# Attention and the SSD half of the output projection in hand-written source order, on one Trainium2 core

## The chip, the core and the metric

The kernel runs on one core of a Trainium2 chip. A core has a matrix engine (TensorE, PE in the profile, with its weight loads as PEld), a vector engine (VectorE, DVE), an activation engine (ScalarE, ACT), a third elementwise engine (GpSimd, POOL), and a queue processor that only starts transfers (SyncE, SP). Each engine has a stream of instructions of its own. Operands lie in the core's SRAM; TensorE writes its sums to PSUM banks, and weights and some intermediate tensors travel to and from DRAM by DMA. The metric is the device time of one execution in microseconds (us); smaller is better.

## What is computed

One block of a hybrid model for 512 tokens of 2048 features, all in fp32. Cut to what matters:

```python
def reference(x, attn_norm_w, w_in, ..., w_out, ffn_norm_w, w_gate, w_up, w_down, final_norm_w):
    h = x
    u = rmsnorm(h, attn_norm_w)                                   # 512 x 2048
    z, xbc, dt, q, kc, vc, ks, vs, kw, vw, gate = split(u @ w_in) # in-projection, 2048 x 5184
    y_ssd = ssd_mixer(z, xbc, dt, ...)          # conv, chunked state space, rmsnorm(y * silu(z)): 512 x 1024
    y_att = nsa_mixer(q, kc, vc, ks, vs, kw, vw, gate, ...)       # 16 heads of 64, 4 key groups: 512 x 1024
    mixed = concatenate([y_ssd, y_att])
    h = h + mixed @ w_out                                         # out-projection, 2048 x 2048
    v = rmsnorm(h, ffn_norm_w)
    h = h + (silu(v @ w_gate) * (v @ w_up)) @ w_down              # FFN
    return rmsnorm(h, final_norm_w)
```

`nsa_mixer` adds three gated attentions: over 31 compressed keys (two small matrix products, w1 and w2, make them from kc and vc), over selected blocks and over a window. With 512 tokens the latter two are plain causal attentions with their own keys (branch 0: ks, vs; branch 1: kw, vw).

## The kernel before

**Split products.** Every fp32 operand is split into a high part and a remainder (`a_hi` on ACT, `lo` on DVE or POOL, the helpers at L120 and L123), and a product is three matmuls: high by high, high by low, low by high. A *unit* is 128 columns of a projection for all 512 tokens: 16 k-steps of three matmuls (L227 to L229) into one of two `ps_g` banks; a k-step is a *weight step*. There are 57 units: 41 of the in-projection (the last 19 are, beside three for z, the v, k and q columns of the four key groups) and then 16 of the SSD half of the out-projection with 8 k-steps each. A unit's weights come by SP in chunks of four k-steps (`wraw`), and are split into `whi` (ACT) and `wlo` (DVE), three chunks ahead (LEAD). When a unit is done, its `evac` scales the bank by `rrow` on DVE and goes on: rope and a split for q and k (`ev_q`, `ev_ks`), transposes for v (`ev_vs`), silu and a gate for z (`ev_z`), the residual sum and the squares for the next norm for the out-projection (`ev_os`).

**Ticks.** All work beside the units is written as Python generators under `Sched`: after each weight step `sch.tick()` advances every generator, and a generator says by `yield n` after how many weight steps it wants to go on. `compress` (the w1 and w2 products, L620 to L669) and `attention` are two of them. Attention goes through 32 items for each of four key groups: head h, branch br, row block i of 128 queries against 128(i+1) keys. An item is `score` (two matmuls into one of two `ps_s` banks, L830 and L831, then on DVE the masked maximum at L834, then on ACT the exponential with its sum at L836), `norm` (reciprocal L843 and scaling, on DVE alone or on ACT for branch 0), `trans` (i+1 transposes into one of two `ps_t` banks, L859, then `pth` on ACT and `ptl` on DVE), and after four items `pvmm` (eight matmuls with the values, L875, into the single `ps_v` bank, with the compressed branch at L869 and L870 ahead of branch 0). After two branches the head's output goes to `at`, and each pair of heads is one of eight operands of the second half of the out-projection.

**What sets the order.** In the kernel before, that source order is only the input: the stages up to the second half of the out-projection lie in one block, which the tile framework's list scheduler rearranges by its own simulation of the engines. The second half of the out-projection (L1160 to L1162; its weights are `Z`, loaded by SP, and `R`, split off on ACT) and the FFN come behind, in an order written by hand under `tc.manual_schedule()`. `pre_out` runs ahead of the first out-projection unit; it loads the eight gated SSD outputs `gy_d` and splits them.

The main loop of before, at the end of the body, is

```python
    for n, u in enumerate(units):
        if n == 4:
            ...
        run_unit(u)
    run_rest()
```

Of the kernel before, what the change touches and what calls it, by code (L numbers as in the profile page):

```python
# [26 lines left out]
KSUB = 4  # L27
PACE = [1]
LAG = 3
EB = 5  # L30
LEAD = 3
# [79 lines left out]
def body(ctx, tc, xT, w_in, w_out, w_gate, w_up, w_down, w1k, w1v, cols, rows, kst, out):  # L111
# [60 lines left out]


    subs = []

    class Unit:
        def __init__(self, src, nk, rhs, evac, need=(), pre=None, cols=(0, 512)):
            self.cols, self.rhs, self.evac, self.need, self.pre, self.nk = cols, rhs, evac, need, pre, nk
            self.sub = []
# [5 lines left out]
    st = {"dma": 0, "split": 0}  # L185
# [10 lines left out]
    def issue_split(upto):  # L196
        while st["split"] <= min(upto, len(subs) - 1):
# [3 lines left out]
            h = wp.tile([128, KSUB, 128], F32R, tag="whi", name="whi", bufs=4)  # L201
            l = wp.tile([128, KSUB, 128], F32R, tag="wlo", name="wlo", bufs=4)
            a_hi(h[:, :n, :], raw[i][:, :n, :])
            lo(dve, l[:, :n, :], raw[i][:, :n, :], h[:, :n, :])
            hi_t[i], lo_t[i] = h, l
            del raw[i]
            st["split"] += 1
            issue_dma(i + 3)

    def run_unit(u):  # L210
# [9 lines left out]
        for i, k0, n in u.sub:  # L220
            issue_split(i)
            for j in range(n):
                if j == 0:
                    issue_split(i + LEAD)
                k = k0 + j
# [4 lines left out]
                sch.tick()  # L230
            del hi_t[i], lo_t[i]

        def evac():
            yield from u.evac(p)
            sch.flags.add(("evac", n_u))
# [307 lines left out]
    def ev_z(t):  # L543
        def ev(p):
# [11 lines left out]
            else:  # L556
                yield from sch.wait("att")
                sp = pools["att"][1]
# [3 lines left out]
                mul(dve, zs, p, rrow)  # L562
                act.activation(zs, zs, AF.Silu)
                mul(pool, zs, zs, y)
            nc.gpsimd.dma_start(gy_d[t], zs)
            if t == 0:
                act.activation(acc2, zs, AF.Square)
            else:
                sq = sp.tile([128, 512], F32, tag="sq" if g == 0 else "yz", name="sq", bufs=1)
                act.activation(sq, zs, AF.Square)  # L570
                add(pool, acc2, acc2, sq)
            sch.flags.add(("gy", t))
# [105 lines left out]
    def ev_vs(g):  # L678
        def ev(p):
            yield from sch.wait("r1", "att")  # L680
            ap = pools["att"][1]
# [3 lines left out]
            yield from after(("a", g - 2))  # L685
            q = ps_m()
            for i in range(4):
                pe.transpose(q[:, i * 128:(i + 1) * 128], t[:, i * 128:(i + 1) * 128], ident)
            v = ap.tile([128, 4, 2, 128], F32R, tag="v", name="v", bufs=2)
            for br in range(2):  # L690
                s = q.rearrange("p (i b d) -> p i b d", i=4, b=2)[:, :, br, :]
                a_hi(v[:, :, br, 0:64], s)
                lo(dve, v[:, :, br, 64:128], s, v[:, :, br, 0:64])
# [17 lines left out]
    def rope2(ap, sw, ro):  # L711
        t = ap.tile([128, 512], F32, tag="fo", name="ro2", bufs=1)
# [3 lines left out]
    def ev_ks(g):  # L716
        def ev(p):
            yield from sch.wait("r1", "att")
            ap = pools["att"][1]
            t = ap.tile([128, 512], F32, tag="qs", name="kt", bufs=2)  # L720
            mul(dve, t, p, rrow)
            sw, ro = rope(ap, t)
            yield 4
            rope2(ap, sw, ro)
            yield from after(("a", g - 2))
            kh = ap.tile([128, 2, 512], F32R, tag="kh", name="kh", bufs=2)
            kl = ap.tile([128, 2, 512], F32R, tag="kl", name="kl", bufs=2)
            for br in range(2):
                s = ro[br * 64:br * 64 + 64, :]
                own = slice(br * 64, br * 64 + 64)  # L730
                for r in range(2):
                    d = slice(r * 64, r * 64 + 64)
                    a_hi(kh[d, br, :], s)
                for r in range(2):
                    d = slice(r * 64, r * 64 + 64)
                    lo(dve if r == br else pool, kl[d, br, :], s, kh[own, br, :])
            R["k", g] = (kh, kl)
# [3 lines left out]
    def q_stack(ap, tag, bufs, s, eng):  # L741
        t = ap.tile([128, 2, 512], F32R, tag=tag, name=tag, bufs=bufs)
        a_hi(t[0:64, 0, :], s[0:64, :])
        a_hi(t[64:128, 1, :], s[64:128, :])
        lo(eng, t[64:128, 0, :], s[0:64, :], t[0:64, 0, :])
# [3 lines left out]
    def ev_q(g, j):  # L749
        def ev(p):  # L750
            yield from sch.wait("r1", "att")
            ap = pools["att"][1]
            t = ap.tile([128, 512], F32, tag="qs", name="qt", bufs=2)
            mul(dve, t, p, rrow)
            sw, ro = rope(ap, t)
            uq = q_stack(ap, "uq", 1, t, pool)
            yield 2
            yield from after(("sc", g - 2))
            if j == 0:
                R["sc", g] = ap.tile([128, 4, 4, 32], F32, tag="sc", name="sc", bufs=2)  # L760
            m = ps_m()
            pv = m[:, 0:256].rearrange("p (i h k) -> p i h k", i=4, h=2)
            for i in range(4):
                for h in range(2):
                    st_ = uq[:, h, i * 128:(i + 1) * 128]
                    pe.matmul(pv[:, i, h, :], st_, kch[:, g, :], start=True, stop=False)
                    pe.matmul(pv[:, i, h, :], st_, kcl[:, g, :], start=False, stop=True)
            dve.tensor_tensor(R["sc", g][:, :, 2 * j:2 * j + 2, :], pv,
                              cmask[:, :, None, :].to_broadcast([128, 4, 2, 32]), ALU.add)
            yield 2  # L770
            rope2(ap, sw, ro)
            if (g, j) == (3, 1):
# [4 lines left out]
                sch.flags.add("x")  # L777
            yield from after(("h", g - 1 if j else g - 2, 1 if j else 3))
            R["rq", g, j] = q_stack(ap, "rq", 3, ro, dve)
# [3 lines left out]
    def attention():  # L783
# [6 lines left out]
        for g in range(4):  # L790
# [10 lines left out]
                              ALU.subtract)  # L801
            act.activation(sc, sc, AF.Exp, scale=0.125)
            for h in range(4):
                a_hi(vpad[32 * h:32 * h + 32, h, 0:64], vcmp[:, g, :])
                lo(dve, vpad[32 * h:32 * h + 32, h, 64:128], vcmp[:, g, :], vpad[32 * h:32 * h + 32, h, 0:64])
# [10 lines left out]
            sch.flags.add(("sc", g))  # L816
            ch = ap.tile([128, 512], F32R, tag="cph", name="cph", bufs=1)
            cl = ap.tile([128, 512], F32R, tag="cpl", name="cpl", bufs=1)
            a_hi(ch, p)
            lo(dve, cl, p, ch)  # L820
# [4 lines left out]

# [962 lines left out]
```

## Time and profile before

| | |
|---|---|
| median of 3 runs | 2290.25 us (2285.53 to 2290.41) |
| the profiled execution | 2288.18 us |
| its span in the trace | 2286.4 us |
| mean granted TensorE clock | 0.977 of full speed |
| PE busy | 2186.6 us, 96% of the span |
| DVE busy | 1804.6 us, 79% |
| ACT busy | 1091.9 us, 48% |
| POOL busy | 431.1 us, 19% |

The span is counted from its own start, and all places below are us from there. The last unit matmul starts at 777.42, the second half of the out-projection at 800.12, and the FFN takes the rest. A matmul's recorded duration is longer than the spacing of matmuls, since they are pipelined; where work is counted, the spacing is used. A wait is put down to the releaser that came last. The granted clock is a mean over a stretch: it is 1.00 at 2.4 GHz and 0.5 at 1.2 GHz, and values between are a mixture.

### The profile page before, as it was taken

The numbers are of one execution on the slowest core, as the hardware profiler recorded it, in microseconds if no ns is written. First come the engines' busy times: TensorE is split into PE (matmuls) and PEld (weight loads), VectorE is DVE, ScalarE is ACT, GpSimd is POOL, SyncE is SP. The second block draws the span as 40 slices with busy tenths as digits, with TensorE's granted clock in tenths as the row PEclk, the third lists the DMA queues.
The fourth block names the chain that finished last, engine by engine and source line by source line (L and its number), as shares of the span: only waits on it lengthen the run. The fifth ranks groups of instructions, "written<-read, shape, count | busy, mean of one in ns | idle before, by whom it ended". The sixth has DMA issues, their size and how long they took to land. (4 is left out here: it accounts for less than half of the span.)

```text
span 2286.4 us, 39808 instructions
## 1 busy us (share of the span) xinstructions
PE 2186.6 (96%) x15376; PEld 2039.4 (89%) x15376; DVE 1804.6 (79%) x2921; ACT 1091.9 (48%) x1770; POOL 431.1 (19%) x436
## 2 busy tenths in 40 slices
PE   7999999999989899999999999999999698989997
PEld 5888888888868678999999999999999698989996
DVE  7699766688888667888887888888887687878786
ACT  4564446566766544444444444444444233333353
POOL 2011334223233133100000000000001121212132
PEclk8999999999999899999999999999999899999998
DMA  5222343222424265878787887878788758677776
GB/s 176 92 70 77 129 135 104 69 85 74 135 63 137 73 226 158 244 218 243 213 255 220 249 227 221 238 218 244 220 255 255 285 173 264 207 241 234 247 169 168
DMA packets 151693, 417.87 MB, mean 183 GB/s; under 512 B 16352, under 2 KB 22000, under 8 KB 151504
## 3 DMA queue, kind: packets, MB, share of 16 engines
q1 hardware_dynamic: 99408, 251.25, 31.6%
q0 software_dynamic: 25536, 77.05, 17.5%
q10 hardware_dynamic: 26560, 87.04, 10.6%
q8 instruction: 120, 1.97, 0.3%
q14 instruction: 69, 0.57, 0.1%
HBM read 353.93 MB, written 57.41 MB: 180 GB/s over the span
## 5 line engine op out<-in xcount | busy, mean ns | idle before, releaser
L120 ACT ACTIVATE R<-Z 128x1024 fp32r<-128x1024 f32 (+4 forms) x488 | 441.9, 922 | 575.0 <-DVE Z L129 324.6
L123 DVE TENSOR_TENSOR R<-Z,R 128x1024 fp32r<-128x1024 f32 (+4 forms) x381 | 395.2, 1043 | 26.1 <-ACT R L120 20.4
L227 PE MATMUL ps_g<-u,whi 128*128 128x512 f32 x720 | 286.1, 397 | 0.2 <-DVE h L126 0.2
L229 PE MATMUL ps_g<-u,wlo 128*128 128x512 f32 x720 | 284.5, 395 | 0.0
L228 PE MATMUL ps_g<-u,whi 128*128 128x512 f32 x720 | 283.9, 394 | 0.0
L1160 PE MATMUL ps_g<-u,R 128*128 128x256 f32 (+1 forms) x834 | 250.7, 301 | 7.6 <-ACT R L120 7.6
L1161 PE MATMUL ps_g<-u,R 128*128 128x256 f32 (+1 forms) x834 | 249.9, 300 | 0.0
L123 DVE TENSOR_TENSOR wlo<-wraw,whi 128x512 fp32r<-128x512 f32 x196 | 151.3, 775 | 66.5 <-ACT whi L120 65.9
L1162 PE MATMUL ps_g<-u,R 128*128 128x256 f32 (+1 forms) x674 | 200.8, 298 | 0.1
L1160 PE MATMUL ps_t<-u,R 128*128 128x256 f32 x688 | 193.7, 282 | 0.0
L1161 PE MATMUL ps_t<-u,R 128*128 128x256 f32 x688 | 193.5, 281 | 0.0
L1160 PE MATMUL ps_s<-u,R 128*128 128x256 f32 x686 | 193.4, 282 | 0.0
L1161 PE MATMUL ps_s<-u,R 128*128 128x256 f32 x686 | 193.1, 282 | 0.0
L120 ACT ACTIVATE whi<-wraw 128x512 fp32r<-128x512 f32 x196 | 122.5, 626 | 134.2 <-PE ps_g L228 88.5
L1160 PEld LDWEIGHTS ps_g<-u,R 128*128 128x128 f32 x834 | 158.5, 190 | 13.6 <-ACT R L120 7.9
L1161 PEld LDWEIGHTS ps_g<-u,R 128*128 128x128 f32 x834 | 158.6, 190 | 5.9
L1162 PE MATMUL ps_s<-u,R 128*128 128x256 f32 x566 | 160.0, 283 | 0.8 <-DVE R L123 0.8
L229 PEld LDWEIGHTS ps_g<-u,wlo 128*128 128x128 f32 x720 | 135.6, 188 | 27.1
L227 PEld LDWEIGHTS ps_g<-u,whi 128*128 128x128 f32 x720 | 135.9, 189 | 26.0 <-DVE h L126 0.5
L228 PEld LDWEIGHTS ps_g<-u,whi 128*128 128x128 f32 x720 | 135.8, 189 | 25.5
L123 DVE TENSOR_TENSOR E<-Z,R 128x1024 fp32r<-128x1024 f32 x107 | 130.2, 1217 | 5.6 <-ACT R L120 5.5
L1162 PEld LDWEIGHTS ps_g<-u,R 128*128 128x128 f32 x674 | 128.2, 190 | 5.2 <-DVE R L123 1.1
(448 smaller groups left out, 6441.6 us busy)
## 6 DMA issues: line engine op xcount, KB each, us to landing
Z<-in_w_gate SPq DMA_DIRECT2D x96, 512.0 KB, 5.4
Z<-in_w_up SPq DMA_DIRECT2D x94, 512.0 KB, 7.3
wraw<-in_w_in SPq DMA_DIRECT2D x164, 256.0 KB, 3.0
g_d<-A ACTq DMA_DIRECT2D x22, 1792.0 KB, 7.2
u<-g_d ACTq DMA_DIRECT2D x12, 1792.0 KB, 16.3
Z<-in_w_gate POOLq DMA_DIRECT2D x37, 512.0 KB, 7.4
Z<-in_w_up POOLq DMA_DIRECT2D x36, 512.0 KB, 5.6
Z<-in_w_down SPq DMA_DIRECT2D x52, 320.0 KB, 5.7
```

Of the source, the lines that this page charges most:

```text
L120: act.activation(dst, src, AF.Copy, scale=scale)
L123: eng.tensor_tensor(dst, src, f(hi), ALU.subtract)
L227: pe.matmul(p, hi_t[i][:, j, :], ah, start=(k == 0), stop=False)
L228: pe.matmul(p, hi_t[i][:, j, :], al, start=False, stop=False)
L229: pe.matmul(p, lo_t[i][:, j, :], ah, start=False, stop=(k == u.nk - 1))
L1160: pe.matmul(q, h[:, k, :], ah, start=(k == 0), stop=False)
L1161: pe.matmul(q, h[:, k, :], al, start=False, stop=False)
L1162: pe.matmul(q, l[:, k, :], ah, start=False, stop=(k == s.blk.n - 1))
```

## The change

From the unit of the first v columns (unit 23 of 57) to the last but one, each unit and all that its weight steps advance run under `tc.manual_schedule()`: the instructions then stand on each engine in the order in which the Python code issues them. The scheduler still orders what lies ahead of unit 23 and, apart from it, the last unit with the rest of its generators.

The source order itself is written anew:

- An attention item is cut into twelve stages, each issued a stated number of weight steps after the item's score: maximum 1, exponential 2, scaling 4 and 5, transposes 7, `pth` 8, `ptl` 9, value matmuls 11, output 13 to 15. An item starts every two weight steps. A group of 32 items takes 2x32+15 = 79 weight steps; before it took 72.
- The split of a weight chunk is divided: `whi` is issued at the first k-step of a chunk and `wlo` at its third.
- The evacuations have more `yield`s between an instruction and its consumer on another engine, and each starts one weight step later. `hold` keeps two generators from using one single buffer at once.
- The loads and splits of `gy_d` move from `pre_out` into `ms_hook`, called after each k-step of the last in-projection unit (unit 41).

The main parts of the diff:

```diff
@@ run_unit
         for i, k0, n in u.sub:
-            issue_split(i)
+            issue_low(i)
             for j in range(n):
                 if j == 0:
                     issue_split(i + LEAD)
+                if j == 2:
+                    issue_low(i + LEAD)
...
                 sch.tick()
+                if u.hook:
+                    u.hook(k)
...
         def evac():
+            yield 1
             yield from u.evac(p)
@@ attention
             n = len(items)
-            for s in range(n + LAG + 1):
-                if s < n:
-                    score(*items[s])
...
-                yield 1
-                if 0 <= s - LAG < n:
-                    trans(*items[s - LAG])
-                if s < n:
-                    norm(*items[s])
-                yield PACE[s % len(PACE)]
-                if 0 <= s - LAG - 1 < n and items[s - LAG - 1][2] == 3:
-                    pvmm(*items[s - LAG - 1][:2])
+            stages = {0: score, 1: top, 2: expo, 4: norm, 5: norm2, 7: trans, 8: high, 9: low, 11: pvmm, 13: out_a,
+                      14: out_b, 15: out_c}
+            for t in range(2 * n + 15):
+                for d in sorted(stages, reverse=True):
+                    if (t - d) % 2 == 0 and 0 <= (t - d) // 2 < n:
+                        stages[d](*items[(t - d) // 2])
                 yield 1
@@ pre_out and ms_hook
+    def ms_hook(k):
+        if k == 0:
+            sch.run_until(*[("gy", t) for t in range(8)])
+            P2["ms"] = [(U[:, 0, i], U[:, 1, i]) for i in range(8)]
+        if k < 8:
+            nc.sync.dma_start(f(U[:, 1, k]), gy_d[k])
+        k -= 6
+        if 0 <= k < 8:
+            a_hi(U[:, 0, k], f(U[:, 1, k]), scale=col(C_SN + k))
+        k -= 1
+        if 0 <= k < 8:
+            dve.scalar_tensor_tensor(U[:, 1, k], f(U[:, 1, k]), col(C_SN + k), f(U[:, 0, k]), op0=ALU.mult,
+                                     op1=ALU.subtract)
@@ main loop
-        run_unit(u)
+        if order.index(U_VS[0]) <= n < len(units) - 1:
+            if u.pre:
+                u.pre()
+                u.pre = None
+            if n == len(order) - 1:
+                u.hook = ms_hook
+            with tc.manual_schedule():
+                run_unit(u)
+        else:
+            run_unit(u)
```

Where the change moves instructions is told here for TensorE at three places. In the changed kernel the unit matmuls are L241 to L243, the w1 products L643 to L645, the scores L883 and L884, the transposes L926, the value matmuls L949, the norm's sums and their transposes L292 and L302, and the second half of the out-projection L1252.

TensorE near the end of `compress`, before: the last products with w1 (L620 to L622) stand between the matmuls of unit 23.

```order
L229 MATMUL ps_g<-u,wlo 128x512
L227 MATMUL ps_g<-u,whi 128x512
L620 MATMUL ps_s<-w1h,xh 124x256
L228 MATMUL ps_g<-u,whi 128x512
L229 MATMUL ps_g<-u,wlo 128x512
L621 MATMUL ps_s<-w1l,xh 124x256
L622 MATMUL ps_s<-w1h,xl 124x256
```

The same place in the changed kernel, at the last matmul of unit 22:

```order
L242 MATMUL ps_g<-u,whi 128x512
L643 MATMUL ps_s<-w1h,xh 124x256
L243 MATMUL ps_g<-u,wlo 128x512
L655 MATMUL ps_t<-ident,hd 124x128 x2
L644 MATMUL ps_s<-w1l,xh 124x256
L645 MATMUL ps_s<-w1h,xl 124x256
```

The L243 here is the last unit matmul for 79 rows. The last four of the eight pairs of w1 chunks and the w2 products stand in these rows alone, and unit 23 begins behind them; before, three of these pairs stood among matmuls of unit 23.

TensorE behind unit 43 (the second unit of the out-projection), before: the end of unit 43 is followed by 114 rows of attention matmuls without a unit matmul.

```order
L227 MATMUL ps_g<-u,whi 128x512
L228 MATMUL ps_g<-u,whi 128x512
L229 MATMUL ps_g<-u,wlo 128x512
L830 MATMUL ps_s<-kh,rq 128x512
L831 MATMUL ps_s<-kl,rq 128x512
L830 MATMUL ps_s<-kh,rq 128x128
L831 MATMUL ps_s<-kl,rq 128x128
L869 MATMUL ps_v<-cph,vpad 128x512
L870 MATMUL ps_v<-cpl,vpad 128x512
L859 MATMUL ps_t<-ident,e 128x128 x7
```

The same units in the changed kernel, in unit 43:

```order
L884 MATMUL ps_s<-kl,rq 128x512
L926 MATMUL ps_t<-ident,e 128x128
L241 MATMUL ps_g<-u,whi 128x512
L242 MATMUL ps_g<-u,whi 128x512
L243 MATMUL ps_g<-u,wlo 128x512
L943 MATMUL ps_v<-cph,vpad 128x512
L944 MATMUL ps_v<-cpl,vpad 128x512
L949 MATMUL ps_v<-pth,v 128x512
L241 MATMUL ps_g<-u,whi 128x512
```

Attention's matmuls now stand between the weight steps of units 42 to 54; the first two rows shown end a stretch of 24 rows without unit matmuls (10 ticks in which unit 43 waits until the unit two ahead is evacuated).

TensorE at the start of the second half of the out-projection, before:

```order
L859 MATMUL ps_t<-ident,e 128x128 x2
L285 MATMUL ps_m<-ident,rst 128x128 x4
L859 MATMUL ps_t<-ident,e 128x128 x7
L875 MATMUL ps_v<-pth,v 128x512
L875 MATMUL ps_v<-ptl,v 128x512
L875 MATMUL ps_v<-pth,v 128x384
L875 MATMUL ps_v<-ptl,v 128x384
L875 MATMUL ps_v<-pth,v 128x256
L875 MATMUL ps_v<-ptl,v 128x256
L875 MATMUL ps_v<-pth,v 128x128
L875 MATMUL ps_v<-ptl,v 128x128
L1160 MATMUL ps_g<-u,R 128x512
```

and in the changed kernel:

```order
L241 MATMUL ps_g<-u,whi 128x512
L242 MATMUL ps_g<-u,whi 128x512
L243 MATMUL ps_g<-u,wlo 128x512
L292 MATMUL ps_m<-ones,acc_95 128x1 x4
L302 MATMUL ps_m<-ident,rst 128x128 x4
L1252 MATMUL ps_g<-u,R 128x512
```

Attention's last value matmuls now stand 42 unit matmuls ahead of the last one, and behind the units only the sums for the norm are left. The first load of `Z` on SP waits for the last sum into `at` in both kernels.

## Rows read from the trace of the kernel before

**Rows 1.** Busy time of the engines in stretches of 20 us; the columns are named in the first line.

```profile
core 0: us, PE busy (x) PEld busy (x) DVE busy (x) ACT busy (x) POOL busy (x), PEclk, DMA share, GB/s
...
320.00:340.00 20.00, 18.34 (x107) 15.33 (x106) 9.21 (x19) 8.07 (x20) 5.55 (x9) 0.91 0.27 86
...
600.00:620.00 20.00, 20.00 (x100) 16.85 (x99) 18.84 (x47) 15.40 (x35) 0.94 (x2) 1.00 0.55 183
620.00:640.00 20.00, 17.78 (x119) 14.86 (x117) 17.88 (x60) 15.40 (x41) 5.67 (x5) 1.00 0.21 67
640.00:660.00 20.00, 15.85 (x69) 13.01 (x70) 17.51 (x48) 13.16 (x34) 8.55 (x10) 0.83 0.06 18
660.00:680.00 20.00, 16.76 (x85) 13.64 (x84) 14.40 (x43) 12.11 (x31) 3.95 (x5) 1.00 0.36 117
680.00:700.00 20.00, 17.07 (x85) 13.72 (x84) 17.60 (x48) 14.66 (x37) 8.32 (x8) 0.91 0.36 108
...
780.00:800.00 20.00, 10.39 (x48) 8.01 (x46) 8.23 (x20) 7.97 (x17) 1.60 (x3) 0.68 0.24 74
```

**Rows 2.** What TensorE waited for between 330 and 800: line, releaser, us in total, times, longest.

```profile
PE ps_s L830 <- DVE em L834: 9.9, 9, 2.4
PE ps_v L869 <- DVE at L129: 2.3, 2, 1.5
```

**Rows 3.** Timeline of TensorE at 647 to 655: start, us, engine, line, operation; in brackets the idle time before and its releaser.

```profile
647.24 0.48 PE L830 MATMUL ps_s<-kh,rq 128*128 128x128 f32 x1 [2.36 <-DVE em L834]
...
654.44 0.47 PE L227 MATMUL ps_g<-u,whi 128*128 128x512 f32 x1
```

**Rows 4.** Timeline of TensorE at the end of `compress`: the first product of each of the last four pairs of w1 chunks, the last matmul of unit 23, and the start of unit 24.

```profile
308.03 0.28 PE L620 MATMUL ps_s<-w1h,xh 128*124 128x256 f32 x1
...
314.44 0.28 PE L620 MATMUL ps_s<-w1h,xh 128*124 128x256 f32 x1
...
320.88 0.28 PE L620 MATMUL ps_s<-w1h,xh 128*124 128x256 f32 x1
...
328.01 0.28 PE L620 MATMUL ps_s<-w1h,xh 128*124 128x256 f32 x1
...
328.36 0.40 PE L229 MATMUL ps_g<-u,wlo 128*128 128x512 f32 x1
...
333.82 0.78 PE L227 MATMUL ps_g<-u,whi 128*128 128x512 f32 x1
334.39 0.63 PE L228 MATMUL ps_g<-u,whi 128*128 128x512 f32 x1
```

**Rows 5.** The raw w1 tiles between 297 and 332: the splits that free them, the loads on POOL, and the time from a load's issue to its landing.

```profile
L123 DVE TENSOR_TENSOR w1l<-w1r,w1h x10: 675/693/1430, 296.9 to 324.8; 128x512 fp32r<-128x512 f32 x10
...
L602 POOL DMA_DIRECT2D w1r<-in_w1v x8: 546/546/563, 297.9 to 319.3; - x8
...
DMA to landing us min/median/max: 3.0/3.0/4.6
```

**Rows 6.** Timeline of all engines around the end of the units: the last unit matmul and the work up to the first matmul of the second half of the out-projection.

```profile
777.19 0.39 PE L228 MATMUL ps_g<-u,whi 128*128 128x512 f32 x1
777.42 0.39 PE L229 MATMUL ps_g<-u,wlo 128*128 128x512 f32 x1
...
777.90 0.69 DVE L126 TENSOR_TENSOR h<-ps_g,rrow 128x512 f32<-128x512 f32 x1
...
778.74 1.27 POOL L129 TENSOR_TENSOR h<-h,sw 128x512 f32<-128x512 f32 x1 [4.26 <-DVE h L126]
...
780.37 0.62 ACT L996 ACTIVATE sw<-h 128x512 f32<-128x512 f32 x1
...
781.21 0.68 DVE L129 TENSOR_TENSOR at<-ps_v,fo 64x512 f32<-64x512 f32 x1
...
781.81 0.67 DVE L129 TENSOR_TENSOR acc<-acc,sw 128x512 f32<-128x512 f32 x1
...
782.54 1.05 PE L275 MATMUL ps_m<-ones,acc 128*128 128x1 f32 x8
...
784.24 0.15 DVE L276 TENSOR_SCALAR rst<-ps_m 128x4 f32<-128x4 f32 x1
...
784.49 1.03 POOL L281 TENSOR_TENSOR rst<-rst,colc 128x4 f32<-128x4 f32 x1 [3.62 <-DVE rst L276]
...
788.09 1.06 PE L285 MATMUL ps_m<-ident,rst 128*128 128x128 f32 x4
...
793.96 0.69 DVE L129 TENSOR_TENSOR at<-ps_v,fo 64x512 f32<-64x512 f32 x1 [1.96 <-ACT fo L883]
794.68 2.42 SPq L1102 DMA_DIRECT2D Z<-in_w_out  x4
...
800.12 0.80 PE L1160 MATMUL ps_g<-u,R 128*128 128x512 f32 x1 [6.82 <-ACT R L120]
```

**Rows 7.** Groups of DVE instructions between 621 and 700, by line and shape: busy us, mean ns of one.

```profile
L123 DVE TENSOR_TENSOR ptl<-ps_t,pth 128x512 fp32r<-128x512 f32 x8 | 5.5, 685 | 0.0
...
L123 DVE TENSOR_TENSOR wlo<-wraw,whi 128x512 fp32r<-128x512 f32 x8 | 5.4, 687 | 3.7 <-ACT whi L120 3.7
...
L834 DVE CUSTOM_DVE_ANT_0 e<-ps_s,kc 128x128 f32<-128x128 f32 x8 | 2.3, 285 | 1.1 <-PE ps_t L859 1.0
...
L123 DVE TENSOR_TENSOR ptl<-ps_t,pth 128x128 fp32r<-128x128 f32 x7 | 2.0, 281 | 0.0
```

More of the change, by code (lines that the diff above doesn't have):

```diff
@@ L171, in body, with hold @@
     wp = open_pool("wp")
+    held = set()
+    def hold(what):
+        while what in held:
+            yield 1
+        held.add(what)
     subs = []
@@ L200, in issue_split, with issue_low @@
             n = subs[i][1]
[L201 to L205, printed above, removed]
+            hi_t[i] = wp.tile([128, KSUB, 128], F32R, tag="whi", name="whi", bufs=4)
+            a_hi(hi_t[i][:, :n, :], raw[i][:, :n, :])
+            st["split"] += 1
+    def issue_low(upto):
+        issue_split(upto)
+        while st["low"] <= min(upto, len(subs) - 1):
+            i = st["low"]
+            n = subs[i][1]
+            lo_t[i] = wp.tile([128, KSUB, 128], F32R, tag="wlo", name="wlo", bufs=4)
+            lo(dve, lo_t[i][:, :n, :], raw[i][:, :n, :], hi_t[i][:, :n, :])
             del raw[i]
-            st["split"] += 1
+            st["low"] += 1
             issue_dma(i + 3)
@@ L557, in ev @@
                 yield from sch.wait("att")
+                yield from hold("qv")
                 sp = pools["att"][1]
@@ L680, in ev @@
             yield from sch.wait("r1", "att")
+            yield from hold("qv")
             ap = pools["att"][1]
@@ L685, in ev @@
             yield from after(("a", g - 2))
+            yield from hold("m")
             q = ps_m()
@@ L711, in rope2 @@
     def rope2(ap, sw, ro):
+        yield from hold("fo")
+        held.remove("fo")
         t = ap.tile([128, 512], F32, tag="fo", name="ro2", bufs=1)
@@ L718, in ev @@
             yield from sch.wait("r1", "att")
+            yield from hold("ro")
             ap = pools["att"][1]
@@ L751, in ev @@
             yield from sch.wait("r1", "att")
+            yield from hold("ro")
             ap = pools["att"][1]
@@ L760, in ev @@
                 R["sc", g] = ap.tile([128, 4, 4, 32], F32, tag="sc", name="sc", bufs=2)
+            yield from hold("m")
             m = ps_m()
@@ L804, in attention @@
                 a_hi(vpad[32 * h:32 * h + 32, h, 0:64], vcmp[:, g, :])
+            yield 2
+            for h in range(4):
                 lo(dve, vpad[32 * h:32 * h + 32, h, 64:128], vcmp[:, g, :], vpad[32 * h:32 * h + 32, h, 0:64])
@@ L986, in ev @@
             if c == 0:
+                yield from hold("m")
                 yield from rms_stats(acc2, 1024, rrow, "r2")
+                held.remove("m")
             yield from sch.wait("r2", "x")
```

135 lines of the change are left out of this document (89 added, 46 removed).

## The prediction

> **What bounds the kernel now.** I read the busy time by stretches first. TensorE is busy for 20.00 of 20 us in nearly all of the units' time; it falls short at the end of `compress` (18.34 at 320), between 620 and 700, and around 780 to 800, where 10.39 are left [rows 1]. So the program is a queue of matmuls with three leaks, and a reordering can win only there. The list of waits says what leaks: between 330 and 800 the costliest is a score matmul that waits for the bank which the maximum on DVE still reads, 9.9 us in nine waits [rows 2]. The timeline shows its form: 2.36 us idle ahead of a score, and the next unit matmul only at 654.44 [rows 3]. DVE is busy there for 17.9 and 17.5 of 20 us: attention alone, without units between it, is bounded by DVE. The last leak is a chain, from the last unit matmul at 777.42 to the first matmul of the second half at 800.12 [rows 6].
>
> **What the leaks cost.** I count matmuls at their spacing in full-clock rows (0.23 us for 512 columns [rows 6], in proportion for fewer, and 0.11 for 128). A unit of 16 steps is 48 x 0.23 = 11.0 us, one of 8 steps 5.5. Counted in this way the 358 matmuls of the four stretches from 620 to 700 make 56.5 us of work, in 80 us: 23.5 lost. 12.5 of them show as idle time in the four stretches (80 less 67.5 busy); most of the rest is half clock, 0.83 and 0.91 granted [rows 1], which the matmuls show as 0.63 and 0.78 us in place of 0.39 where the same happens at 333.82 [rows 4]. The units from 24 on hold 424.3 us of work, with 4.2 us of the end of `compress`; the last matmul of unit 23 is over at 328.6 [rows 4], and 328.6 + 424.3 + 24.7 lost = 777.6, so the count closes: 23.5 here, 1.2 at the end of `compress`. Then come 22.5 us to 800.1.
>
> **The change, part by part.**
>
> *Attention between the units.* The matmuls that stood alone behind unit 43 and behind the last unit now stand between weight steps. I count DVE's work as I count TensorE's, by the spacing of its instructions: one begins some 0.08 us before the recorded end of the one ahead (0.68 at 781.21, the next at 781.81 [rows 6]). An item brings DVE a maximum and a `ptl` (0.28 to 0.68 each, by the size of the item [rows 7]) and small work for the scaling, on average 1.3 us by spacing. A unit of 8 steps carries four items; with two `wlo` of 0.69 [rows 7] and three sums and products of 0.68 that makes 7.5 to 8.6 us, against 9.1 to 9.6 on TensorE (5.5 and four items of 0.95). But where DVE bounded, between 620 and 660, it was busy for only 35.4 of 40 us [rows 1], 0.885 of the time, since it also waits for ACT. By this factor it needs 8.5 to 9.7 us a unit, even with TensorE: over units 46 to 54 the new order takes DVE to the edge and not over it.
>
> Four units are denser. By the order, the DVE work that stands beside unit 42 makes 17.0 us (seven items, three splits of `gy_d`, three `wlo`, the end of the last q), with the factor 19.2, against 12.6 on TensorE; unit 41 has 20.5 and so 23.2 against 20.7, unit 36 20.1 and 22.7 against 22.4, unit 43 11.7 and 13.2 against 13.0. That is 6.6 + 2.5 + 0.3 + 0.2 = 9.6 us of stalls. From below it is 4, unit 42 without the factor. From above it is 26: recorded durations in full, 20.9, 24.9, 24.7 and 14.7 us in these four (16.5 over TensorE) and 0.4 to 0.8 over it in each of some fifteen others. The stretches of ticks without a weight step, eight with 28 ticks, add small waits: 3 us, by the 1.5 us of a longest wait of this kind [rows 2], 1 to 6. I take 13 in all, 5 to 32.
>
> *The end of `compress`.* Here the change takes cover away. Unit 23 ran between the last three pairs of w1 chunks, and now stands behind them. These pairs came 6.4, 6.5 and 7.1 us apart [rows 4]; POOL starts a load only when `w1l` has freed the raw tile, and it lands 3.0 us later, 4.6 at most [rows 5]; then come the splits, 0.7 us on DVE for each of two chunks [rows 5] and about as much on ACT, and 1.4 us of matmuls, twelve of 0.12. So the chain is mostly its own: without unit matmuls ahead of them I give a pair 6 us. In the new order the pairs also begin 18 unit matmuls later, 4.1 us. The last pair starts at 328.0 + 4.1 less 3 x 0.7, at 330; `compress` ends at 335 in place of 333.1 (331 with 5 us a pair, 338 with the old pace and half clock in the pairs' own matmuls). But 11.0 us of unit matmuls are still to come that were done before. The restart at half clock [rows 4] stays: 1.7 us by the doubled spacing of the first eight or so matmuls.
>
> *The end of the units.* Only the last unit's chain stays: product on DVE 0.69, sum on POOL 1.27, square 0.62, sum 0.67, the matmuls 1.05 (eight of them recorded there, at most that), rst 0.15, POOL 1.03 and the four transposes, 1.06 at half clock [rows 6]: 6.6 us and some 0.1 at each of eight handovers, 7.5, and about 1 us until the first product runs. The load of `Z` waits for the last `at`, at 793.96 before [rows 6]; now it comes some 13 us ahead of the last unit matmul, and `R` needs 5.5 us from then (794.68 to 800.12): hidden by the units and the chain, with 15 us to spare. The 6.7 us of attention matmuls in the old tail move between the units.
>
> *The divided weight split, the evacuations, the hook.* They change no count. `wlo` stands two steps behind `whi`, still two chunks ahead of its use. The eight loads of `gy_d` go through SP among the weights, one per step; SP waits for the raw weight tiles anyway. I price them at nothing; their cover is the lead of three chunks, 8 us of matmuls, and one missed chunk would cost a load of about 3 us.
>
> *The sum.* TensorE's work behind `compress`: 424.3 - 4.2 + 11.0 + 6.7 = 437.8. Then 335 + 1.7 + 437.8 + 13 + 7.5 + 1 = 796.0, against 800.1: 4.1 us earlier. The FFN and all behind is the same code in the same hand order. The profiled execution took 2288.2 us and would take 2284.1; the median of the runs, 2290.25, lies 2 above it, inside their spread. I take 2284.
>
> **A rule that speaks against the change.** A stalled score holds back all that follows it: at 647.24 TensorE idled while unit matmuls stood behind it, ready since their weights were split, until 654.44 [rows 3]. In the Trainium skill, "TensorE: Matmul & The Clock Gate", section "The mechanism", the same is stated as a rule: matmuls start and end strictly in program order, and only weight loads are pulled ahead. By that rule a source order without any look at durations could be worse than the scheduler's, and the trace agrees as far as this wait shows it; what it would give here is the second rival.
>
> **The rivals.**
>
> *The uncovered chain eats the gain: about 2289.* If the pairs keep 6.7 us each and their matmuls run at half clock, `compress` ends at 338 or later; with stalls of 15 the second half starts at 801. For it speaks that the pairs were evenly spaced before [rows 4] though unit matmuls of very different number stood between them; against it, that the last pair's splits then waited for the matmuls of the pair before, which now come sooner.
>
> *Order without slack: slower, about 2303.* Mechanism: each `ps_s` and `ps_t` bank is one of two, so a maximum or a `ptl` that DVE reaches over two weight steps (about 2 us) late stops TensorE, unit matmuls included. It decides if DVE needs its recorded durations in full: 26 by the count above, and 6 for the waits between engines, 32 in place of 13, 19 later: 2303. For it: DVE was busy 18.84 of 20 at 600 without a stall of TensorE, and 17.9 with one [rows 1], so it saturates near there, and the new order needs as much of it in several stretches. Against it: all its consumers now stand two or more weight steps behind.
>
> *Nearly all hidden: about 2273.* Stalls of 5 and a `compress` that ends at 332: 11 us less than my sum. For it: DVE's and ACT's stages lie a weight step apart, so no wait between engines is in series with TensorE.
>
> *The change does not do what it says* would mean that attention still stands alone somewhere; the order shows that it does not, so this has no chance worth a number.
>
> **How the numbers follow.** My own sum, faster by about 0.27%, 0.38; the uncovered chain, within 0.2%, 0.24; order without slack 0.20; nearly all hidden 0.18. About 0.2%, 4.6 us, is what a measurement of this kernel tells from no change, and my sum lies just beyond it, so a quarter of its chance is "same", and a little of it "slower". Faster 0.46, same 0.31, slower 0.23. The ends: compress at 331 and stalls of 5 give 2272; a price of 32 for the stalls gives 2303. The range, cut by the least likely of both sides, is 2271 to 2302; the likeliest case's own is 2279 to 2289.
>
> **What would show it.** Right: between 620 and 700 no stretch under 18 us of TensorE in 20; the first unit matmul behind `compress` at about 335 and the second half at about 796, some 8 us behind the last unit matmul; waits of a score for the maximum mostly around units 41 to 43, under 15 us. Wrong: granted clock under 0.9 within units 29 to 54, or many waits below 1 us spread over them (the second rival); a gap of over 25 us between units 22 and 23 (the first). Wrong altogether would be a longer FFN, since nothing in it is changed.

## The result and the profile after

The changed kernel took 2312.01 us (median of 4 runs, 2308.61 to 2315.75), the kernel before 2287.89 beside it: slower by a ratio of 1.0111, 95% interval 1.0098 to 1.0124, some 25 us. The forecast was 2284 and the range ended at 2302. The profiled execution has a span of 2311.7 us.

First the stretches of 20 us, the columns as in [rows 1], from the changed kernel:

```profile
320.00:340.00 20.00, 14.26 (x69) 11.17 (x70) 7.41 (x13) 7.99 (x19) 2.55 (x5) 0.57 0.28 93
...
380.00:400.00 20.00, 14.92 (x72) 12.06 (x71) 11.14 (x21) 8.26 (x16) 6.76 (x6) 0.92 0.21 70
400.00:420.00 20.00, 19.58 (x90) 15.81 (x89) 11.93 (x41) 14.76 (x34) 3.16 (x3) 0.91 0.31 106
...
500.00:520.00 20.00, 14.77 (x59) 11.66 (x57) 13.24 (x28) 8.60 (x18) 3.13 (x3) 0.83 0.25 79
...
640.00:660.00 20.00, 19.85 (x116) 17.09 (x115) 18.97 (x50) 18.45 (x43) 10.64 (x10) 1.00 0.41 139
660.00:680.00 20.00, 16.12 (x89) 12.91 (x87) 19.41 (x54) 16.32 (x39) 5.14 (x6) 1.00 0.22 70
680.00:700.00 20.00, 15.40 (x72) 12.89 (x73) 11.98 (x40) 11.44 (x28) 5.44 (x5) 0.75 0.23 80
...
820.00:840.00 20.00, 14.90 (x61) 12.30 (x62) 7.53 (x9) 7.16 (x10) 5.09 (x5) 0.83 0.54 178
```

Before, TensorE had no loss between 340 and 600, and the stretches from 620 to 700 leaked [rows 1]. Now there are two new holes, at 380 and at 500, each with a granted clock under 1; the leak from 620 on has shrunk to 660 to 700; and the hole at the end of `compress` is over three times as deep: TensorE is idle for 5.7 of 20 us in place of 1.7, at a granted clock of 0.57 in place of 0.91. Next what TensorE waited for between 340 and 830, as in [rows 2]:

```profile
PE ps_g L241 <- ACT whi L118: 8.0, 5, 3.2
PE ps_m L292 <- DVE acc L127: 4.7, 1, 4.7
PE ps_t L926 <- DVE ptl L121: 4.4, 4, 2.6
PE ps_t L864 <- DVE sc L124: 3.9, 2, 2.0
PE ps_v L949 <- DVE ptl L121: 3.2, 5, 1.1
```

The score's wait for the maximum, 9.9 us before [rows 2], is gone. In its place unit matmuls wait for `whi` (the high part of their own weights) and the four transposes of the compressed softmax (L864) for `sc`; neither wait is in the list of before. The hole at 380 is made of these two. The timeline there, of TensorE, DVE and ACT, the rows that matter:

```profile
387.37 0.39 PE L241 MATMUL ps_g<-u,whi 128*128 128x512 f32 x1
...
389.61 0.69 DVE L124 TENSOR_TENSOR zs<-ps_g,rrow 128x512 f32<-128x512 f32 x1 [4.33 <-PE ps_g L243]
...
390.34 0.63 ACT L582 ACTIVATE zs<-zs 128x512 f32<-128x512 f32 x1 [4.61 <-DVE zs L124]
...
390.87 0.62 ACT L118 ACTIVATE whi<-wraw 128x512 fp32r<-128x512 f32 x1
...
391.51 1.28 ACT L849 ACT_TABLE_LOAD   x1
...
391.77 0.69 DVE L843 TENSOR_REDUCE sm<-sc 128x16 f32<-128x512 f32 x1
...
392.81 0.39 PE L243 MATMUL ps_g<-u,wlo 128*128 128x512 f32 x1
...
393.68 0.63 ACT L849 ACTIVATE sc<-sc 128x512 f32<-128x512 f32 x1 [0.89 <-DVE sc L845]
394.22 1.07 ACT L118 ACTIVATE vpad<-vcmp 32x64 fp32r<-32x64 f32 x4
...
395.32 0.63 ACT L118 ACTIVATE whi<-wraw 128x512 fp32r<-128x512 f32 x1
...
396.00 0.50 PE L241 MATMUL ps_g<-u,whi 128*128 128x512 f32 x1 [2.80 <-ACT whi L118]
...
397.89 0.69 DVE L124 TENSOR_TENSOR sc<-sc,sm 128x512 f32<-128x512 f32 x1
...
398.64 0.69 PE L864 MATMUL ps_t<-ident,sc 128*128 128x128 f32 x2 [1.91 <-DVE sc L124]
```

Read it from the end. The transposes at 398.64 wait for a chain that began at 391.77 on DVE: maximum, difference, exponential on ACT, sum, scaling: 6.8 us, 398.58 less 391.77. The source sets the transposes nine weight steps behind the first of these. At this place no item is under way, so a weight step is three unit matmuls, 0.69 us, and nine are 27 unit matmuls or 6.2 us; where items run, nine steps would be some 10 us, by the prediction's 0.95 us for an item and an item every two steps.

The chain also began late. The 27th unit matmul ahead of the transposes is the one at 387.37, and DVE came to the maximum 4.4 us behind it: the product of a z unit stood ahead of it on DVE and waited until 389.61 for its last matmul (4.33 us idle), and then two splits for q took 1.4 us. Late start and length together, 4.4 and 6.8 us, are 11.2 us where the source leaves 6.2, and the two waits of TensorE inside, 2.80 and 1.91, make up nearly all of the difference. The `whi` of 395.32, for which the unit matmul of 396.00 waits, stands on ACT behind the chain's exponential.

The length alone stops nothing. For the third key group the chain takes 6.8 us again, over the same 27 unit matmuls without an item, and the transposes start without a wait, since DVE began 0.8 us ahead of the first of these matmuls, the one at 605.72:

```profile
604.89 0.68 DVE L843 TENSOR_REDUCE sm<-sc 128x16 f32<-128x512 f32 x1
...
605.72 0.39 PE L241 MATMUL ps_g<-u,whi 128*128 128x512 f32 x1
...
611.03 0.69 DVE L124 TENSOR_TENSOR sc<-sc,sm 128x512 f32<-128x512 f32 x1
...
611.88 0.63 PE L864 MATMUL ps_t<-ident,sc 128*128 128x128 f32 x4
```

The end of `compress` and the first unit matmul behind it, on TensorE ([rows 4] before):

```profile
330.81 0.26 PE L690 MATMUL ps_s<-w2vh,hh 128*32 128x64 f32 x1 [0.98 <-ACT hh L118]
...
334.16 0.79 PE L241 MATMUL ps_g<-u,whi 128*128 128x512 f32 x1 [1.50 <-ACT whi L118]
334.75 0.63 PE L242 MATMUL ps_g<-u,whi 128*128 128x512 f32 x1
```

`compress` is over at 332.6, and unit 23 starts at 334.16, close to the forecast (335 for both, and half clock). Last the end of the units ([rows 6] before):

```profile
817.68 0.39 PE L243 MATMUL ps_g<-u,wlo 128*128 128x512 f32 x1
...
819.28 0.69 DVE L124 TENSOR_TENSOR h<-ps_g,rrow 128x512 f32<-128x512 f32 x1 [2.15 <-DMA h_d<-h]
820.11 1.26 POOL L127 TENSOR_TENSOR h<-h,sw 128x512 f32<-128x512 f32 x1 [3.95 <-DVE h L124]
...
822.81 1.46 PE L292 MATMUL ps_m<-ones,acc 128*128 128x1 f32 x8 [4.74 <-DVE acc L127]
...
826.56 1.11 PE L302 MATMUL ps_m<-ident,rst 128*128 128x128 f32 x4 [2.29 <-POOL rst L298]
827.33 0.78 PE L1252 MATMUL ps_g<-u,R 128*128 128x512 f32 x1
```

From the end of the last unit matmul (817.9) to the second half pass 9.4 us, where 22.5 were: the expected gain is there. But the second half starts at 827.3 in place of 800.1. From 334.16 to 817.9 are 483.7 us for the 437.8 us of matmuls that the prediction counted: 45.9 lost, where it had 13 and 1.7 for the restart. Counted by spacing in the same way, 24.7 of these lie between the ends of units 24 and 40 (358 to 643 us), 14.7 in units 41 to 43, and some 3 behind them; the rest is the restart and the rounding of the count. Behind 827.3 the program takes 1484.4 us to the end of the span; before it took 1486.3 behind 800.1.

One thing of the change the part on it above told wrongly. A hand-ordered region keeps its own instructions in order on each engine, and each unit has a region of its own; how two regions lie against each other is left to the scheduler. It puts neighbouring units into each other: by the buffer numbers in the order, TensorE has 24 matmuls of unit 25, 14 of unit 26, the other 24 of unit 25, and so on up to unit 56. So the changed kernel is not in source order across units. The first experiment asks what that costs. The unit number told there is one too high as well: in the list of units the first v columns are unit 22, where the regions begin and from which the experiments count; the last units of the in-projection are 20, four of them for z.

### The profile page after: what moved, and what is told of

It is laid out like the page before. It is cut to its first block, busy times and chain, and to the rows that moved or that the text cites. A ratio compares the mean times of both kernels' runs of the same rounds, so it can differ in the third digit from the quotient of the medians.

```text
span 2311.7 us, 39742 instructions
## 1 busy us (share of the span) xinstructions
PE 2196.5 (95%) x15376; PEld 2039.8 (88%) x15376; DVE 1809.7 (78%) x2921; ACT 1091.2 (47%) x1768; POOL 422.2 (18%) x435
## 5 line engine op out<-in xcount | busy, mean ns | idle before, releaser
L241 PE MATMUL ps_g<-u,whi 128*128 128x512 f32 x720 | 301.1, 418 | 9.5 <-ACT whi L118 9.5
L242 PE MATMUL ps_g<-u,whi 128*128 128x512 f32 x720 | 284.3, 395 | 0.0
L243 PE MATMUL ps_g<-u,wlo 128*128 128x512 f32 x720 | 284.3, 397 | 0.0
L1252 PE MATMUL ps_g<-u,R 128*128 128x256 f32 (+1 forms) x834 | 250.5, 300 | 0.7 <-ACT R L118 0.7
L1252 PE MATMUL ps_t<-u,R 128*128 128x256 f32 x688 | 194.0, 282 | 0.0
L1252 PE MATMUL ps_s<-u,R 128*128 128x256 f32 x686 | 193.7, 282 | 0.0
L121 DVE TENSOR_TENSOR wlo<-wraw,whi 128x512 fp32r<-128x512 f32 x196 | 145.9, 748 | 46.1 <-ACT whi L118 45.4
L241 PEld LDWEIGHTS ps_g<-u,whi 128*128 128x128 f32 x720 | 137.7, 191 | 33.1 <-ACT whi L118 11.4
L1252 PEld LDWEIGHTS ps_g<-u,R 128*128 128x128 f32 x834 | 158.3, 190 | 6.6 <-ACT R L118 0.9
L243 PEld LDWEIGHTS ps_g<-u,wlo 128*128 128x128 f32 x720 | 136.7, 190 | 30.7 <-DVE wlo L121 0.7
L1253 PEld LDWEIGHTS ps_g<-u,R 128*128 128x128 f32 x834 | 158.3, 190 | 5.9
L127 DVE TENSOR_TENSOR Z<-Z 128x1024 f32<-128x1024 f32 (+5 forms) x119 | 126.2, 1061 | 8.3 <-POOL Z L127 5.3
```

Of the source, the lines that this page charges most:

```text
L121: eng.tensor_tensor(dst, src, f(hi), ALU.subtract)
L127: eng.tensor_tensor(o, a, b, ALU.add)
L241: pe.matmul(p, hi_t[i][:, j, :], ah, start=(k == 0), stop=False)
L242: pe.matmul(p, hi_t[i][:, j, :], al, start=False, stop=False)
L243: pe.matmul(p, lo_t[i][:, j, :], ah, start=False, stop=(k == u.nk - 1))
L1252: pe.matmul(q, h[:, k, :], ah, start=(k == 0), stop=False)
```

## The experiments

All times are medians; the ratios are to the kernel before, run beside each on the same chip, with 95% intervals. Not all experiments ran on one chip, so a difference between two of them is given by the medians and, where it matters, by the ratios too.

### One region for all units

```diff
+    region, FIRST = ExitStack(), order.index(U_VS[0])
     for n, u in enumerate(units):
...
+        if n == FIRST:
+            region.enter_context(tc.manual_schedule())
...
-            with tc.manual_schedule():
-                run_unit(u)
+        if n == len(units) - 1:
+            region.close()
+        run_unit(u)
```

Expected: 

> The changed kernel with one hand-ordered region from unit 22 to unit 56 in place of one region per unit: the order between units is the source's too. Theory A (the seams): in the changed kernel the scheduler lays the chains of two neighbouring units into each other, so an evacuation comes late and the weight splits on ACT and DVE stand behind it; the 30 us lost at units 26 and 27, 33, 42 and 43 are lost there. Expected 2288 (2282 to 2295), and the waits of a unit matmul for whi under 3 us in place of 9.5. Rival B (no slack): the source order itself is late at the start of a key group, where the compressed softmax and the evacuations stand in one row on ACT and DVE; expected 2305 to 2318, waits for whi as before.

Measured 2307.08, ratio 1.0084 (1.0069 to 1.0099). Some 5 us less than the changed kernel, near the limit of the intervals: theory A, that the seams (the borders between regions) are the loss, fell. Its waits of TensorE between 340 and 830:

```profile
PE ps_t L864 <- DVE sc L124: 6.5, 3, 3.3
PE ps_v L949 <- DVE ptl L121: 4.4, 4, 1.6
PE ps_t L926 <- DVE ptl L121: 3.8, 2, 2.6
PE ps_m L808 <- POOL uq L121: 3.8, 4, 1.2
```

The wait for `whi` is gone, as A had it and not B, but the softmax's wait has grown from 3.9 to 6.5 us, and most of the loss has stayed. So most of the cause lies in the source order itself.

### The region begins two units later

```diff
-    region, FIRST = ExitStack(), order.index(U_VS[0])
+    region, FIRST = ExitStack(), order.index(U_VS[0]) + 2
```

Expected: 

> As the kernel with one region, but the region begins two units later, so that units 22 and 23 are placed by the scheduler between the last products with w1, as in the kernel before. By both theories the uncovered end of compress costs about 10 us (unit 23 took 35.1 us in the changed kernel for 20.7 us of matmuls): expected 8 to 12 less than the kernel with one region, so 2278 by A and 2296 to 2308 by B. If the scheduler loses as much elsewhere, no gain.

Measured 2292.47, ratio 1.0031 (1.0017 to 1.0045): 14.6 us less than with the region from unit 22 by the medians, 12 by the ratios, where both theories had 8 to 12. The stretch from 320 to 340 is that of before again:

```profile
320.00:340.00 20.00, 17.99 (x110) 15.05 (x109) 11.04 (x23) 8.83 (x21) 5.22 (x10) 0.91 0.25 80
```

This is the cover that the prediction priced.

### No region, and the old source in a region

```diff
-        if order.index(U_VS[0]) <= n < len(units) - 1:
...
-            with tc.manual_schedule():
-                run_unit(u)
-        else:
-            run_unit(u)
+        if n == len(order) - 1:
+            u.hook = ms_hook
+        run_unit(u)
```

Expected: 

> The new source (stages one weight step apart, hook, divided split), with no hand-ordered region: the list scheduler places all. Theory A and B alike: about the kernel before, 2284 to 2298, since the scheduler decides the order there; compress covered again, the attention tail and the stretch behind unit 43 back. If it is as slow as the changed kernel (2305 and more), the loss is in the new source and not in the order.

Measured 2289.90, ratio 1.0015 (1.0005 to 1.0024). Under the scheduler the new source is some 3 us slower than the old one; the loss is in the order. Then the kernel before, its own source, with the lines of the first experiment put around its unit loop:

Expected: 

> The kernel before, with its old source, in one hand-ordered region from unit 22 to unit 56. A score, its maximum and its exponential stand there in one weight step, the scaling one step later, the transposes with both copies in one. Theory: without the stages each step's chain is in series on ACT and DVE and stops TensorE, 1 us or more for each of 128 items: over 2400. If the stages matter little, it is within 10 us of the kernel with one region.

Measured 2517.32, ratio 1.1001 (1.0984 to 1.1017). The old source in its own order costs 230 us, and its list of waits between 320 and 1040 is headed by waits inside an item and by one of the evacuations for q:

```profile
PE ps_v L875 <- ACT pth L120: 49.9, 18, 6.9
PE ps_s L830 <- DVE em L834: 34.9, 11, 5.1
PE ps_m L766 <- POOL uq L123: 34.4, 14, 5.6
```

In a hand-ordered region the new source is 210 us faster. How much of that is the stages, and how much the later evacuations, the divided split and the hook, was not taken apart.

### The softmax spaced

On the kernel with one region from unit 24:

```diff
             mul(dve, sc.rearrange("p i h k -> p (i h) k"), ...)
-            yield 6
+            yield 12
             p = ps_t()
```

Expected: 

> As the kernel with one region from unit 24 (2292.5), with one number changed: the transposes of the compressed softmax at the start of a key group are issued 12 weight steps behind its sums, not 6. Theory C (chains at a group's start): that softmax, alone on DVE and ACT with nothing but unit matmuls on TensorE, takes longer than six weight steps, and stops TensorE for 3.3 us at 385 and at 496, each time followed by half clock. Expected 7 to 10 less, 2283 to 2286, and no wait of these transposes. Rival D (density): the later start of the group's items moves work towards units 42 and on, where DVE bounds, and gives back all but 3 us.

Measured 2284.52, ratio 0.9986 (0.9976 to 0.9996): 8 us less by the medians and 10 by the ratios, as theory C had it. The softmax's transposes no longer stand in its list of waits:

```profile
PE ps_t L926 <- DVE ptl L121: 5.6, 6, 1.8
PE ps_v L949 <- DVE ptl L121: 4.4, 7, 2.0
PE ps_m L808 <- POOL uq L121: 3.1, 3, 1.2
PE ps_g L1252 <- ACT R L118: 2.8, 1, 2.8
```

### Less work for DVE in units 41 and 42

On the same kernel with one region from unit 24, the low operands of the SSD half stay raw:

```diff
-        k -= 1
-        if 0 <= k < 8:
-            dve.scalar_tensor_tensor(U[:, 1, k], f(U[:, 1, k]), col(C_SN + k), f(U[:, 0, k]), op0=ALU.mult,
-                                     op1=ALU.subtract)
```

Expected: 

> As the kernel with one region from unit 24 (2292.5), with the eight remainder splits of gy_d on DVE left out (the low operands of the SSD half hold the raw values). They lie in units 41 and 42. Theory D (density, the prediction's second rival): units 41 to 43 are bounded by DVE's total, 6.2 us less of it gives 4 to 6 us: 2287 to 2289. Theory C: the waits there are chains at the boundary of the out-projection (the norm's sums, the evacuation ahead of unit 43), and the total does not matter: 2291 to 2293.

Measured 2288.61, ratio 1.0007 (0.9997 to 1.0018), 4 us less by the medians and 5.5 by the ratios, as theory D had it by number; the intervals of the two kernels just touch. But the traces do not put the gain where D has it. From the end of unit 40 to the end of unit 43 the kernel with the splits takes 59.6 us (627.5 to 687.1) and this one 58.7 (624.9 to 683.6): 0.9 us less, for 6.2 us less work on DVE. So D is not shown: by these two traces, what stops TensorE there is mostly something else than DVE's total.

### Both repairs in the changed kernel itself

With one region per unit as in the changed kernel, first each repair alone, then both.

```diff
+    FIRST = order.index(U_VS[0]) + 2
...
-        if order.index(U_VS[0]) <= n < len(units) - 1:
+        if FIRST <= n < len(units) - 1:
```

Expected: 

> The changed kernel (one region per unit), with the first region two units later, at unit 24: units 22 and 23 cover the end of compress again. Measured with one region this was worth 14.6 us. If it is the cover alone, 2297 (2294 to 2300) here; if the scheduler's seams eat it, over 2303.

Measured 2299.49, ratio 1.0054 (1.0037 to 1.0071): 12.5 us less than the changed kernel, as for the cover alone. The softmax alone, `yield 12` in place of `yield 6`:

Expected: 

> The changed kernel (one region per unit), with the compressed softmax's transposes 12 weight steps behind its sums, not 6. Worth 8 us with one region. In the changed kernel TensorE waits at units 27 and 33 first for whi (2.8 and 3.2 us), then for the softmax (1.9 and 2.0): if both come from the softmax chain that stands ahead on ACT, 2303 to 2305; if the wait for whi is the seam's own, only about 4 us, 2307 to 2309.

Measured 2299.95, ratio 1.0057 (1.0042 to 1.0072): 12 us, more than either case had. The list of waits between 340 and 830 shows why:

```profile
PE ps_g L241 <- ACT whi L118: 1.5, 2, 1.2
PE ps_t L864 <- DVE sc L124: 1.5, 2, 1.0
```

The wait for `whi` has fallen from 8.0 to 1.5 with the softmax's, though nothing was done to it: with regions per unit, the late softmax costs in two places. The 1.5 us of the transposes (0.95 and 0.58) that are left fit the account too: a late start of 4.4 and 4.0 us and a chain of 6.9 meet 10.4 us of weight steps. Both repairs:

Expected: 

> The changed kernel with both: regions per unit from unit 24, softmax spaced by 12. With one region both together gave 2284.5. If the seams cost 5 us as between the changed kernel and one region, 2288 to 2291; then cover, softmax chain and seams explain the loss against the kernel before. If they cost more than 10, one of the two effects needs the one region.

Measured 2285.59, ratio 0.9994 (0.9985 to 1.0003). The two add up: 12.5 and 12.1 us alone, 26.4 together. With both done, one region (0.9986) and regions per unit (0.9994) have overlapping intervals: a cost of the seams as such can't be told from none (1 us by the medians, 2 by the ratios).

### The hand order only where the scheduler loses

The new source, one region that begins at unit 41, and one that begins at unit 37:

```diff
-    region, FIRST = ExitStack(), order.index(U_VS[0])
+    region, FIRST = ExitStack(), len(order) - 1
...
-    region, FIRST = ExitStack(), order.index(U_VS[0])
+    region, FIRST = ExitStack(), order.index(U_VS[3]) - 1
```

Expected: 

> The new source with the list scheduler up to unit 40 and one hand-ordered region from unit 41. Up to 620 the scheduler lost nothing beside units (kernel before and the kernel with no region), and the hand order gains only in the out-projection. Its lag piles up in unit 41: 33.7 us of matmuls beside 37.7 us of DVE work there, some 9 lost. Expected second half at 791 to 796 and 2274 to 2280, below the kernel before. If the piled-up lag costs more than 20, about 2290.

Measured 2285.70, ratio 0.9994 (0.9984 to 1.0004): no measurable gain; the forecast missed. The second half starts at 799.1. Unit 41, where attention's lag piles up, ends at 639.7 and loses 13 us by spacing where the forecast had 9, and units 42 and 43 lose 13 more, which uses up what the order gives behind them.

Expected: 

> As the last, with the region from unit 37, the last z unit: the pile is smaller there, 31.0 us of matmuls beside 31.2 of DVE, some 4 lost, while units 38 to 40 are hand-ordered without loss by the trace of the kernel with one region (12.7, 14.0 and 18.8 us for as much work). Expected 3 to 6 less than the kernel with the region from unit 41: 2270 to 2276.

Measured 2282.66, ratio 0.9979 (0.9969 to 0.9989): 3 us less than from unit 41, as expected, though the two intervals overlap; both lie some 6 to 7 us above the end of their forecasts. The last kernel adds the softmax's 12 steps:

Expected: 

> One region from unit 37 (2282.7) with the softmax spaced by 12. Only the last key group's softmax lies in the region, where TensorE waited 0.9 us for it; its items start six weight steps later, which moves DVE work out of units 42 and 43. Expected 2278 to 2283: no loss, a gain of 2 to 4 if units 42 and 43 are bounded by DVE.

Measured 2281.51, ratio 0.9976 (0.9967 to 0.9986), the fastest of all; not to be told from the kernel without the 12 steps. It beats the kernel before by 5 to 6 us and the changed one by 30.

## Why the prediction was wrong, point by point

- **The end of `compress`: right.** Forecast 335 and 11.0 us of unit matmuls uncovered behind it; measured 332.6 for its end and, behind a wait of 1.50 us for `whi` that the sum had not, 334.16 for the first unit matmul. Beginning the regions two units later gave 12.5 us (one region: 14.6).
- **The end of the units: right, 0.9 us short.** 9.4 us in place of 7.5 + 1, and 22.5 before. The product of the last unit waited for the write of an earlier `h` to DRAM, which the sum had not: it began 1.60 us behind the start of the last matmul, 0.48 before.
- **The leak from 620 to 700: half right.** The score's wait is gone, but 40 us from 660 to 700 still lose 8.5 us of busy time, and the clock was 0.75 in the second half. The dense units 41 to 43 were seen, but the price, 9.3 us by DVE's total (2.5, 6.6 and 0.2), had the wrong size and the wrong reason: by spacing they lose 0.5, 4.9 and 9.3 us, and taking 6.2 us of DVE work out of the first two shortened the three by 0.9. Most of the loss of unit 43 is one of the stretches of ticks without a weight step, for all eight of which the sum had 3 us: from 682.6 to 694.63 no unit matmul starts, and the first ones behind it run at half clock.

```profile
694.50 0.48 PE L926 MATMUL ps_t<-ident,e 128*128 128x128 f32 x1 [2.63 <-DVE ptl L121]
694.63 0.77 PE L241 MATMUL ps_g<-u,whi 128*128 128x512 f32 x1
```

- **The stalls between units 24 and 40: the step that failed.** The sum had 13 us for all stalls, 9.6 of them the dense units and 3 us for the rest, "small waits, by the 1.5 us of a longest wait of this kind". In the trace all stalls and half clock come to 45.9 us with the restart. That is the whole miss: the second half starts 31.3 us behind the forecast of 796.0, and 45.9 less 14.7 is 31.2. Between units 24 and 40 the sum had 0.3 us for unit 36 and some of the 3; measured are 24.7, of which 21.0 lie from 358 to 421 and from 421 to 533, around the softmax of the first and of the second key group. The term looked for density, and these units are light: DVE is busy for 11.14 and 13.24 of 20 us at 380 and 500. What stopped TensorE there was one late result each time. The compressed softmax began 4.4 and 5.1 us late and needed 6.8 and 6.6 us on two engines, and the source gives it nine weight steps, 6.2 us where no item runs; in the other two groups DVE began ahead of its place, and the same chain stopped nothing. Spaced by 12, it gave back 12 us in the changed kernel, 8 to 10 with one region.
- **What "a weight step" is worth.** The argument against the second rival was that all consumers stand two or more weight steps behind. Slack counted in steps is time only through what a step contains: 0.69 us with no item beside it and some 1.2 with items (half of an item's 0.95 added).
- **What the region does.** The prediction took the whole for one fixed order. With a region per unit it is not, and part of the softmax's lateness turned up as waits for `whi`, a term that the prediction priced at nothing under the lead of three chunks. The order shows how. The unit matmuls that wait at 396.00 are the first two of unit 28, which the scheduler set ahead of the last 18 of unit 27, so their `whi` is wanted 4.1 us earlier than the source has it. And the last matmul of the z unit stands 18 unit matmuls ahead of the softmax's transposes in place of 30, which makes DVE later: 4.4 and 5.1 us in the changed kernel, 1.7 and 2.8 in one region. That was a wrong reading of the change, but a cheap one: about 5 us, and none that can be told once the softmax is spaced.
- **The rivals.** The second, order without slack, had the side right and its mechanism half: a late result in a fixed order stops unit matmuls too, but the late ones were chains at a group's start and not the recorded sum of DVE's durations. Its 2303 is 9 short. The first, the uncovered chain, was in the forecast at its right size already. Of the signs that were named as wrong, one came: a granted clock under 0.9 within units 29 to 54 (0.83 at 500, in units 32 and 33).
- **The rule of the Trainium skill** ("TensorE: Matmul & The Clock Gate", section "The mechanism": matmuls start and end in program order) is what the trace shows at 398.64: the unit matmuls of unit 27 behind L864 were ready and stood still. The prediction's own example was no such case. At 647.24 the unit matmuls could not have run: of the two `ps_g` banks, that of unit 42 was freed only by the product below, at 652.38.

```profile
651.71 0.67 DVE L126 TENSOR_TENSOR h<-ps_g,rrow 128x512 f32<-128x512 f32 x1
```

The account: 1.0111 against 1.0 is 25 us; the cover and the softmax together take away 26.4. The cover's half was in the forecast, the softmax's was not; what it missed besides lies in the half clock behind these waits, in units 41 to 43 and in smaller waits. What is left in the kernel with both, 2285.6, is, by the stretches above, the gain of the tail and the old leak against the dense units and small waits, which nearly cancel; no experiment took these apart. One thing stays open. Of the 44 us lost behind the restart, the list of gaps longer than 0.25 us explains 23.5 and the granted clock up to 12 (next but one section); some 9 us are gaps that the recorded durations of matmuls cover, and were not taken apart.

## What to carry to other kernels

Before an order is fixed by hand, walk the chains that occur once per group, not only the ones in the loop: write down each chain's length from a trace, how late its first engine comes to it, and the time, not the count of steps, that lies between its ends at that place. Look at what the scheduler had laid over an otherwise bare chain (here one unit over the last products with w1), and start the hand order behind it. And take the order over only where the scheduler loses: the region that began at unit 37 beat both kernels, while the one from unit 22 lost more than it gained.

## What the runs showed that was not expected

- The order of the same work on the engines can cost far more than any of its parts: the new source under the scheduler took 2289.9 us, in one region from unit 22 2307.1, and the old source in such a region 2517.3.
- Waits cost more than their length. In the changed kernel the gaps on TensorE between 348 and 818 sum to 23.5 us, the loss to 44. Around the holes the granted clock was 0.92, 0.91, 0.83 and 0.75 over stretches of 20 us; as a mixture of the two levels that is 3.2 + 3.6 + 6.8 + 10.0 = 23.6 us at 1.2 GHz, and, as an estimate, up to 12 us of work lost on top of the waits.
